# Seven accumulating DMAs in place of a matmul: summing the modulation rows of a decoder layer over partitions

## The chip, the cores and the metric

The kernel runs on one core of a Trainium2 chip. Its time is the device time of one execution in microseconds (us); where there are several runs the median is given. Engines are named as in the profile: PE is TensorE (its weight loads are PEld), DVE is VectorE, ACT is ScalarE, POOL is GpSimd, SP is SyncE, which here only issues DMAs. Each engine works through its own instructions in the order in which they were laid down; an instruction that waits holds up all behind it.

## The reference

One decoder layer on x of 512 tokens by 1024 channels. A modulation vector of 6 x 1024 numbers is computed from c; two of its parts scale and shift the first norm, one gates the first residual, two modulate the second norm, one gates the second residual.

```
mod = silu(c) @ w_ada + b_ada                    # 6 x 1024
shift1, scale1, gate1, shift2, scale2, gate2 = split(mod, 6)
h = rmsnorm(x, norm1_g) * (1 + scale1) + shift1
qa, ka, va, qd, kd, vd, ga, gd = split(h @ w_in)
out_a = sliding_window_attention(qa, ka, va, sinks)       # 8 heads of 64, window 128
out_d = diff_attention(qd, kd, vd, lam)                   # 4 heads, two softmax maps each
out_d = rmsnorm(out_d, subln_g) * 0.8                     # per head of 128 columns
merged = sigmoid(ga) * (out_a @ w_branch_swa) + sigmoid(gd) * (out_d @ w_branch_diff)
x = x + gate1 * (merged @ w_out)
h2 = rmsnorm(x, norm2_g) * (1 + scale2) + shift2
x = x + gate2 * conv_ffn(h2)
out = rmsnorm(x, final_g)
```

## The kernel before

All arithmetic is in float32. Large products are made of three matmuls: operands are split into a high part (a cast on ACT, L118) and a low part (a subtraction on DVE, L119), and high x high, high x low and low x high are summed in PSUM.

The kernel has four stages: the norm and the first 768 columns of the input projection (to about 56 us), the two attentions with the rest of the projections (to about 310 us), the output projection and second norm (to about 362 us), and the MLP. The change touches the second stage and the beginning of the third.

**How the second stage is laid out.** The order on PE is written by hand. Projections are cut into units; `fill(n)` (L539) issues n steps of three matmuls each of the current unit, and between the fills stand the attention's scores, transposes and values. `fill` also counts steps ("ticks"): every 8th tick it advances the generator `ada_rows` (L839), and functions put off with `after(n, fn)` run when their count is used up. `flush(kind)` (L569) runs what has been put into the list `beside[kind]`. On the other engines a scheduler decides the order when the kernel is built, by its own estimate of times and by priorities: `tc.high_priority(offset=HP)` moves instructions ahead (HP the most, HP // 2 less), `tc.issue_after(ins)` lets them follow an instruction. PSUM banks are taken by tag: "f" for projections (2), "s" for scores (3), "t" for transposes and small sums (2), "v" (1).

**Modulation rows.** The parts gate1, shift2, scale2 and gate2 (idx 0 to 3) are computed here, each in two halves of 512 (hf 0 and 1), so eight rows; I number them 0 to 7. For each row four loads of 512 KB bring 1024 x 512 weights (L835, `ra`, on SP, into buffers of the tag "raw" that all weight loads of this stage share, four in all), and DVE forms 8 products, each added to the one before (L857, L859, tile `arow`): 128 partitions x 512 partial sums. What remains is a sum over the 128 partitions. `ada_spread` (L872) does it on PE: four matmuls of a 128 x 32 block of ones with 128 columns of `arow`, side by side in the array (L876), fill a bank `pr`; ACT copies it (L881, `row`), and POOL writes 4 x 128 numbers to `mod_rows` in DRAM (L882). The partial sums have two buffers, tags "sq2" and "g2b1"; row 2 therefore takes the buffer of row 0.

**Sliding-window attention.** Four pairs of heads. `swa_scores` puts scores into banks, DVE adds the bias and takes the maxima (L620), `swa_softmax` takes exponentials on ACT (L635), adds the sink (L639, `lsum`), divides on DVE (L644), head j=0 then j=1; `swa_transpose` transposes the quotients on PE (L656, `tp`), ACT copies them (L658), `swa_values` multiplies (L666).

**Differential attention.** Sixteen blocks s = 4 h + n of 128 queries. Scores are read by DVE (L744), exponentials on ACT (L764), quotients of the two maps on DVE (L767 to L769); `diff_transpose` (L781, `td`), whose banks are read by ACT and DVE (L490, L491, `aTh`, `aTl`), and after the fourth block of a head `diff_values` (L124 `od`). The norm of a head: `stats` sums squares on PE (L804, `pss`), DVE forms the mean (L806 to L808, L181), POOL raises it to the power -0.5 (L185, `r`), DVE improves that (L193 to L195, `rt`, `drs`, L810); then `turn_norm` spreads the factors over columns on PE (L815, `rb`) and DVE multiplies (L816). `evac` (L488) reads the banks of q, k and v into the pair of high and low parts (L490, L491, L494).

**After the attention.** `brow` (L1066) loads a row broadcast to 128 partitions, on POOL's queue: gate1 with its bias into `g1b` (L1073, L1074), summed and halved on DVE (L1075, L1076) and multiplied into the output weights (L1105). `m2` gathers shift2, scale2, their biases and norm2_g (L1078 to L1080).

Of the kernel before, what the change touches and what calls it, by code (L numbers as in the profile page):

```python
# [28 lines left out]
ST = 6  # L29
ADA_LAG = 1  # L30
ADA_EVERY = 8
# [23 lines left out]
def kernel(  # L55
# [507 lines left out]

    beside = {"row": [], "sum": [], "norm": [], "turn": []}

    def after(n, fn):
        later.append([n, fn])
# [110 lines left out]
    def add_head(h):  # L678
        def q(wts):
            t = heads[h] = ap.tile([P, 6, S], F32R, tag="qkv", bufs=2, name=f"qkv{h}")  # L680
            o = fbank(f"pq{h}")
            yield from steps(o, wts, hT, KT)
            evac(t[:, 0], t[:, 1], o, 2.0 ** (2 * h - 1))

        def k(wts):
            t = heads[h]
            o = fbank(f"pk{h}")
            yield from steps(o, wts, hT, KT)
            evac(t[:, 2], t[:, 3], o)

        def v(wts):
# [7 lines left out]
            def turn():  # L699
                pv = tbank(f"pv{h}")  # L700
                for m in range(NT):
                    nc.tensor.transpose(pv[:, m * P : (m + 1) * P], vT[:, m * P : (m + 1) * P], ident)
                evac(t[:, 4], t[:, 5], pv)

# [81 lines left out]
    def diff_values(h):  # L786
# [14 lines left out]
        def stats():  # L801
# [37 lines left out]
    def ada_rows():  # L839
# [29 lines left out]
    spread = []  # L869


    def ada_spread(idx, hf, ac):  # L872
        pr = tbank(f"pr{idx}{hf}", (P, P))
        for g in range(4):
            gs = slice(32 * g, 32 * g + 32)
            nc.tensor.matmul(  # L876
                pr[gs], ones[:, gs], ac[:, g * P : (g + 1) * P], start=True, stop=True, tile_position=(0, 32 * g)
            )
        row = big.tile([P, P], F32, tag="g2b0", name=f"row{idx}{hf}")
        with tc.high_priority(offset=HP):  # L880
            spread.append(nc.scalar.copy(row, pr))  # L881
        nc.gpsimd.dma_start(  # L882
            mod_rows[idx, hf * S : (hf + 1) * S].rearrange("(g n) -> g n", g=4), row[0:P:32]
        )

# [3 lines left out]
    def add_gate_a(j):  # L889
# [5 lines left out]
        def load():  # L895
            if j % 2 == 0:
# [19 lines left out]

    group_ahead, sums = [1], {}
    pairs, firsts, scored, probs, aTs = {}, {}, {}, {}, {}
# [16 lines left out]
    for i in range(SWA_PAIRS):  # L935
        more = i + 1 < SWA_PAIRS
        fill(SWA_FILL[3])
        if more:
            flush("row")
            swa_scores(i + 1, range(NT))  # L940
# [10 lines left out]
        if i < 2:  # L951
            flush("row")
            swa_values(i)
        fill(SWA_FILL[7])
    while units or loaded or current:
        fill(1)
    flush("row")
    swa_values(2)
# [9 lines left out]
    for s in range(4 * DIFF_HEADS):  # L968
# [9 lines left out]
        if nxt:  # L978
            flush("row")
# [10 lines left out]
        if s == 13:  # L990
            group_ahead.clear()
        elif s > 13:
            flush("row")
        diff_softmax(*nxt)
# [3 lines left out]
    for j in range(4, KT):  # L998
        add_gate_a(j)
    fill(4)  # L1000
    flush("norm")
# [19 lines left out]
    def add_gate_d(j):  # L1021
# [6 lines left out]
        units.append((lambda: load_cols(win, COL_GD + j * P, f"wgd{j}"), gate))  # L1028

    def add_merge(j):  # L1030
        def load():
# [9 lines left out]
        def branch(wts):  # L1041
# [5 lines left out]
            nc.vector.tensor_add(td, td, ta[:, j])  # L1047
            split(mgh[j], mgl[j], td)

# [15 lines left out]

    def brow(dst, src):  # L1066
        nc.gpsimd.dma_start(dst, src.partition_broadcast(P))

# [9 lines left out]
    nc.gpsimd.dma_start(m2[0:16, :], mod_rows[1:3].rearrange("r (a p) -> (r a) p", p=P))  # L1078
    nc.gpsimd.dma_start(m2[16:32, :], b_ada[0, 3 * D : 5 * D].rearrange("(a p) -> a p", p=P))
    nc.gpsimd.dma_start(m2[32:40, :], norm2_g[0].rearrange("(a p) -> a p", p=P))  # L1080
    pm2 = tbank("pm2", (P, 40))
# [859 lines left out]
```

## Time and profile before

| | |
|---|---|
| Median of 3 runs | 691.77 us (691.5 to 693.38) |
| Profiled execution: time, span | 693.06 us, 691.3 us |
| Granted TensorE clock, mean | 0.996 |
| PE busy | 680.5 us, 98% of the span |
| DVE busy | 565.3 us, 82% |
| ACT busy | 384.6 us, 56% |
| POOL busy | 82.1 us, 12%, 100 instructions |
| DMA | 121.8 MB, q1 (issued by SP) 95.1 MB, q0 (issued by POOL) 25.7 MB |

A row of groups reads: line, engine, operation, tile written <- tiles read, shapes, count | busy time, mean of one | idle time before, and what ended it. A row of a timeline reads: start and duration in us, engine, line, operation, tiles, shapes, count, and in brackets the idle time before it and what ended it. A row of waits reads: engine, its tile and line <- what it waited for: us in total, times, longest. For a DMA, "landing" is the time from its issue until its data are confirmed.

### The profile page before, as it was taken

The page shows a single profiled execution, that of the slowest core. Times are in us where ns is not written, and L with a number is a line of the kernel's source. Part 1 is how long each engine was busy: PE and PEld are TensorE (multiplying, and loading weights), DVE is VectorE, ACT ScalarE, POOL GpSimd, SP SyncE. Part 2 cuts the span into 40 slices and gives each one's busy share as a digit, 9 for nine tenths or more (in the row PEclk, how much of TensorE's full clock was granted, in tenths as well). Part 3 has the DMA queues.
Part 4 walks back from the last instruction along what each step waited for, and adds up shares of the span by engine and source line. Part 5 has one row for each costly group of instructions (what it writes and reads, how often), then busy time and mean ns, then how long its engine had stood idle before and what let it go on. Part 6 is the DMA issues. An engine that isn't in the chain of part 4 may idle for free. (4 is left out here: it accounts for less than half of the span.)

```text
span 691.3 us, 11249 instructions
## 1 busy us (share of the span) xinstructions
PE 680.5 (98%) x4203; PEld 592.7 (86%) x4203; DVE 565.3 (82%) x1073; ACT 384.6 (56%) x686; POOL 82.1 (12%) x100
## 2 busy tenths in 40 slices
PE   8999999999999999999999999999999999999995
PEld 5787877788888888888889999999999999888884
DVE  5898987987885666663789988888888999979997
ACT  7676666545552323332477756655565666656665
POOL 3000000000001000000030101112111002540300
PEclk9999999999999999999999999999999999999998
DMA  9985454553455675229726798777978748997903
GB/s 307 328 258 165 140 156 151 154 163 96 138 138 169 212 217 180 91 95 315 230 56 129 166 214 197 167 173 215 206 215 217 155 149 207 196 195 199 167 1 121
DMA packets 115926, 121.81 MB, mean 176 GB/s; under 512 B 4447, under 2 KB 93344, under 8 KB 115872
## 3 DMA queue, kind: packets, MB, share of 16 engines
q1 hardware_dynamic: 96958, 95.09, 43.8%
q0 software_dynamic: 18720, 25.73, 22.2%
q8 instruction: 33, 0.54, 0.3%
q10 hardware_dynamic: 194, 0.28, 0.1%
q14 instruction: 21, 0.17, 0.1%
HBM read 118.97 MB, written 2.11 MB: 175 GB/s over the span
## 5 line engine op out<-in xcount | busy, mean ns | idle before, releaser
L1270 PE MATMUL up<-t,m_whi 128*128 128x256 f32 x512 | 93.1, 283 | 0.0
L1270 PEld LDWEIGHTS up<-t,m_whi 128*128 128x128 f32 x512 | 79.9, 192 | 0.0
L1270 PE MATMUL up<-t,m_wlo 128*128 128x256 f32 x256 | 72.4, 283 | 0.0
L1270 PE MATMUL up<-bh,p_whi 128*128 128x256 f32 x232 | 65.7, 283 | 0.0
L1270 PE MATMUL up<-bl,p_whi 128*128 128x256 f32 x232 | 65.7, 283 | 0.0
L1270 PE MATMUL up<-bh,p_wlo 128*128 128x256 f32 x232 | 65.7, 283 | 0.0
L859 DVE SCALAR_TENSOR_TENSOR arow<-ra,cs,arow 128x512 f32<-128x512 f32 x56 | 42.0, 749 | 20.0 <-DMA ra<-in_w_ada_dram 19.4
L1270 PEld LDWEIGHTS up<-t,m_wlo 128*128 128x128 f32 x256 | 49.2, 192 | 0.0
L1270 PEld LDWEIGHTS up<-bh,p_whi 128*128 128x128 f32 x232 | 44.5, 192 | 0.0
L1270 PEld LDWEIGHTS up<-bl,p_whi 128*128 128x128 f32 x232 | 44.5, 192 | 0.0
L1270 PEld LDWEIGHTS up<-bh,p_wlo 128*128 128x128 f32 x232 | 44.5, 192 | 0.0
L1179 POOL DMA_DIRECT2D s<-in_w_up_dram x21 | 27.0, 1361 | 140.8 <-DMA s<-in_w_up_dram 66.5
L1207 ACT CAST m_whi<-s 128x1024 fp32r<-128x1024 f32 x31 | 32.5, 1049 | 11.1 <-DVE s L1201 6.3
L1211 DVE TENSOR_TENSOR m_wlo<-s,m_whi 128x1024 fp32r<-128x1024 f32 x31 | 37.8, 1219 | 0.0
L1270 PE MATMUL up<-t,p_whi 128*128 128x256 f32 x176 | 32.2, 283 | 0.0
L882 POOL DMA_DIRECT2D mod_rows<-row x8 | 4.9, 614 | 204.9 <-ACT row L881 204.9
L1270 PEld LDWEIGHTS up<-t,p_whi 128*128 128x128 f32 x176 | 27.5, 192 | 0.0
L1277 ACT ACTIVATE gT<-a,cv 128x512 f32<-128x512 f32 x22 | 17.8, 816 | 16.9 <-DVE a L1312 15.8
L185 POOL TENSOR_TENSOR r<-ms,mhalf 128x1 f32<-128x1 f32 (+1 forms) x16 | 12.6, 791 | 120.9 <-DVE ms L183 73.1
L1207 ACT CAST p_whi<-wa 128x1024 fp32r<-128x1024 f32 x18 | 18.8, 1046 | 12.5 <-PE up L1270 12.5
L1211 DVE TENSOR_TENSOR p_wlo<-wa,p_whi 128x1024 fp32r<-128x1024 f32 x18 | 22.0, 1223 | 3.8 <-ACT p_whi L1207 3.8
L1270 PE MATMUL up<-t,p_wlo 128*128 128x256 f32 x88 | 24.9, 283 | 0.0
(491 smaller groups left out, 2064.9 us busy)
## 6 DMA issues: line engine op xcount, KB each, us to landing
ra<-in_w_ada_dram SPq DMA_DIRECT2D x32, 512.0 KB, 4.4
wa<-in_w_up_dram SPq DMA_DIRECT2D x22, 512.0 KB, 3.9
s<-in_w_up_dram SPq DMA_DIRECT2D x21, 512.0 KB, 4.5
s<-in_w_up_dram POOLq DMA_DIRECT2D x21, 512.0 KB, 6.6
adaw<-in_w_ada_dram SPq DMA_DIRECT2D x12, 512.0 KB, 7.6
w<-in_w_in_dram SPq DMA_DIRECT2D x12, 512.0 KB, 4.9
a<-in_w_up_dram SPq DMA_DIRECT2D x11, 512.0 KB, 4.5
b<-in_w_down_dram SPq DMA_DIRECT2D x10, 512.0 KB, 4.6
```

Of the source, the lines that this page charges most:

```text
L185: nc.gpsimd.tensor_tensor(r0, ms, mhalf[:, :n], ALU.pow)
L859: nc.vector.scalar_tensor_tensor(ac, r[:, a], cc, ac, ALU.mult, ALU.add)
L882: nc.gpsimd.dma_start(mod_rows[idx, hf * S : (hf + 1) * S].rearrange("(g n) -> g n", g=4), row[0:P:32])
L1179: nc.gpsimd.dma_start(dst, upblock(*blk), accum_op=ALU.add)
L1207: nc.scalar.copy(W[J, name][0], R[J, SRC[name]])
L1211: nc.vector.tensor_sub(lo, R[J, SRC[name]], hi.bitcast(F32))
L1270: nc.tensor.matmul(o[u], w[:, k, cu], b[:, k], start=name in ("p1", "m5", "p2") and k == 0 and x == 0, stop=k == 3 and x == 2, skip_group_ ...
L1277: nc.scalar.activation(grow(j), av[J][:, u], AF.Identity, bias=cv[:, 66 + j : 67 + j], scale=cv[:, 44 + j : 45 + j])
```

## The change

The sum over partitions of each modulation row is made by DMAs that accumulate, issued by POOL: the upper half of the partitions is added to the lower half, seven times (64, 32, ... 1 partition), and the first partition is written to `mod_rows`. The matmuls, the bank, ACT's copy and the lists that timed them are gone. The partial sums have three buffers in turn, so row 3 takes the buffer of row 0. The readings of the q and k banks are given a priority of HP * 3 // 4, which lies above that of the rows' products (HP // 2); those of the v bank and the multiplication with the norm factors get HP. The norm factors of the heads before the last are spread two steps after the transposes of a head's second block, where they were spread after the first block's scores had been issued; those of the third head come two steps later. `g1b` and the constant parts of `m2` are loaded on SP's queue, and `g1b` is summed after the second block of the merge. The split of the first branch weights no longer follows a copy of a row.

```diff
-                ac = big.tile([P, S], F32, tag=("sq2", "g2b1")[hf], name=f"arow{idx}{hf}")
+                ac = big.tile([P, S], F32, tag=("sq2", "g2b1", "g2b0")[(2 * idx + hf) % 3], name=f"arow{idx}{hf}")
...
             if k == KT - 2:
-                row = lambda idx=idx, hf=hf, ac=ac: ada_spread(idx, hf, ac)
-                if group_ahead:
-                    beside["row"].append(row)
-                else:
-                    after(ADA_LAG, row)
+                ada_sum(idx, hf, ac)
...
-    def ada_spread(idx, hf, ac):
-        pr = tbank(f"pr{idx}{hf}", (P, P))
-        for g in range(4):
-            gs = slice(32 * g, 32 * g + 32)
-            nc.tensor.matmul(
-                pr[gs], ones[:, gs], ac[:, g * P : (g + 1) * P], start=True, stop=True, tile_position=(0, 32 * g)
-            )
-        row = big.tile([P, P], F32, tag="g2b0", name=f"row{idx}{hf}")
-        with tc.high_priority(offset=HP):
-            spread.append(nc.scalar.copy(row, pr))
-        nc.gpsimd.dma_start(
-            mod_rows[idx, hf * S : (hf + 1) * S].rearrange("(g n) -> g n", g=4), row[0:P:32]
-        )
+    def ada_sum(idx, hf, ac):
+        n = P // 2
+        while n:
+            nc.gpsimd.dma_start(ac[0:n], ac[n : 2 * n], accum_op=ALU.add)
+            n //= 2
+        nc.gpsimd.dma_start(mod_rows[idx : idx + 1, hf * S : (hf + 1) * S], ac[0:1])
...
             yield from steps(o, wts, hT, KT)
-            evac(t[:, 0], t[:, 1], o, 2.0 ** (2 * h - 1))
+            with tc.high_priority(offset=HP * 3 // 4):
+                evac(t[:, 0], t[:, 1], o, 2.0 ** (2 * h - 1))
...
-                nc.vector.tensor_mul(of, of, rb)
+                with tc.high_priority(offset=HP):
+                    nc.vector.tensor_mul(of, of, rb)
...
-                with tc.issue_after(spread[-1].ins) if j == 0 else ExitStack():
-                    pair_w["a"] = split_pair(r, [P, 4, 2 * P], f"wba{j}")
+                pair_w["a"] = split_pair(r, [P, 4, 2 * P], f"wba{j}")
...
         if n == 1:
             diff_transpose(s)
-        fill(DIFF_FILL[2] + ahead)
+            fill(2)
+            flush("norm")
+        fill(DIFF_FILL[2] + ahead - 2 * (n == 1))
         if n == 2:
             flush("sum")
-        elif n == 0:
-            flush("norm")
...
-    fill(4)
+    fill(6)
     flush("norm")
...
-    brow(g1b, mod_rows[0])
-    brow(g1bias, b_ada[0, 2 * D : 3 * D])
-    nc.vector.tensor_add(g1b, g1b, g1bias)
-    nc.vector.tensor_scalar_mul(g1b, g1b, 0.5)
+    brow(g1b, mod_rows[0], nc.sync)
+    brow(g1bias, b_ada[0, 2 * D : 3 * D], nc.sync)
+    with tc.issue_after(merged[1][1].ins):
+        nc.vector.tensor_add(g1b, g1b, g1bias)
+        nc.vector.tensor_scalar_mul(g1b, g1b, 0.5)
     m2 = bp.tile([40, P], F32, name="m2")
+    nc.sync.dma_start(m2[16:32, :], b_ada[0, 3 * D : 5 * D].rearrange("(a p) -> a p", p=P))
+    nc.sync.dma_start(m2[32:40, :], norm2_g[0].rearrange("(a p) -> a p", p=P))
     nc.gpsimd.dma_start(m2[0:16, :], mod_rows[1:3].rearrange("r (a p) -> (r a) p", p=P))
```

More of the change, by code (lines that the diff above doesn't have):

```diff
@@ L29 @@
 ST = 6
-ADA_LAG = 1
 ADA_EVERY = 8
@@ L562, in fill @@
                 next(ada, None)
-    beside = {"row": [], "sum": [], "norm": [], "turn": []}
+    beside = {"sum": [], "norm": [], "turn": []}
     def after(n, fn):
@@ L688, in k @@
             yield from steps(o, wts, hT, KT)
-            evac(t[:, 2], t[:, 3], o)
+            with tc.high_priority(offset=HP * 3 // 4):
+                evac(t[:, 2], t[:, 3], o)
         def v(wts):
@@ L702, in turn @@
                     nc.tensor.transpose(pv[:, m * P : (m + 1) * P], vT[:, m * P : (m + 1) * P], ident)
-                evac(t[:, 4], t[:, 5], pv)
+                with tc.high_priority(offset=HP):
+                    evac(t[:, 4], t[:, 5], pv)
             if h:
@@ L815, in turn_norm @@
                     nc.tensor.transpose(rb[:, n * P : (n + 1) * P], rs[:, n : n + 1].to_broadcast([P, P]), ident)
-                nc.vector.tensor_mul(of, of, rb)
+                with tc.high_priority(offset=HP):
+                    nc.vector.tensor_mul(of, of, rb)
                 split(outd[0][:, h], outd[1][:, h], of)
@@ L915, in add_gate_a @@
         units.append((load, branch))
-    group_ahead, sums = [1], {}
+    sums = {}
     pairs, firsts, scored, probs, aTs = {}, {}, {}, {}, {}
@@ L938 @@
         if more:
-            flush("row")
             swa_scores(i + 1, range(NT))
@@ L951 @@
         if i < 2:
-            flush("row")
             swa_values(i)
@@ L956 @@
         fill(1)
-    flush("row")
     swa_values(2)
@@ L978 @@
         if nxt:
-            flush("row")
             diff_scores(*nxt)
@@ L982 @@
             diff_transpose(s)
-        fill(DIFF_FILL[2] + ahead)
+            fill(2)
+            flush("norm")
+        fill(DIFF_FILL[2] + ahead - 2 * (n == 1))
         if n == 2:
             flush("sum")
-        elif n == 0:
-            flush("norm")
         if n != 1:
             diff_transpose(s)
[L990 to L993, printed above, removed]
         diff_softmax(*nxt)
@@ L1028, in add_gate_d @@
         units.append((lambda: load_cols(win, COL_GD + j * P, f"wgd{j}"), gate))
+    merged = []
     def add_merge(j):
@@ L1047, in branch @@
             nc.vector.tensor_add(td, td, ta[:, j])
-            split(mgh[j], mgl[j], td)
+            merged.append(split(mgh[j], mgl[j], td))
         units.append((load, branch))
@@ L1063, with brow @@
     man.close()
-    def brow(dst, src):
-        nc.gpsimd.dma_start(dst, src.partition_broadcast(P))
+    def brow(dst, src, q=nc.gpsimd):
+        q.dma_start(dst, src.partition_broadcast(P))
     TAIL = 3
```

3 lines of the change are left out of this document (removed).

## The prediction

> **What bounds the kernel now.** I read the page first (engine shares, chain), then TensorE's waits in the stretch the change touches (56 to 345 us), then the timelines of single engines there.
>
> ```profile
> span 691.3 us, 11249 instructions
> PE 680.5 (98%) x4203; PEld 592.7 (86%) x4203; DVE 565.3 (82%) x1073; ACT 384.6 (56%) x686; POOL 82.1 (12%) x100
> PE tp L656 <- DVE st L644: 0.5, 1, 0.5
> 125.00:150.00 25.00, 25.00 (x138) 19.84 (x137) 22.12 (x63) 13.88 (x35) 0.58 (x1) 1.00 0.55 166
> 225.00:250.00 25.00, 25.00 (x119) 20.30 (x118) 15.79 (x20) 8.49 (x11) 2.13 (x4) 1.00 0.69 217
> ```
>
> TensorE is busy for 98% of the span. In the third line, the only row of its waits between 56 and 345 us, it waits once, 0.5 us, for the softmax quotients of the last window pair. So two things count: TensorE work removed is worth its own length, and anything that makes VectorE late can only cost. The last two lines are stretches of 25 us (busy TensorE, its weight loads, VectorE, ScalarE, POOL, the granted clock, the DMA share): VectorE has room after 200 us (15.79 of 25) but little where softmax feeds transposes (22.12). The time is made against the profiled execution's own 693.06 us, which lies 1.29 above the median 691.77; I give the time as the median plus the sum.
>
> **Removed from TensorE.** Eight groups of eight records (four matmuls each), with their copies.
>
> ```profile
> L876 PE MATMUL pr<-arow,ones x64: 272/285/298, 108.9 to 283.7; 128*32 128x128 f32 x64
> 131.65 0.39 PE L123 MATMUL pA<-outal,wba_h 128*128 128x512 f32 x1
> 131.87 0.40 PE L124 MATMUL pA<-outah,wba_l 128*128 128x512 f32 x1
> 132.20 0.43 PE L876 MATMUL pr<-arow,ones 128*32 128x128 f32 x8
> 132.55 0.95 PE L129 MATMUL sd<-qkv 64*128 64x128 f32 x12
> ```
>
> By starts, a group holds TensorE 0.35 us (132.20 to 132.55), and the matmul ahead takes 0.33 instead of 0.22 us before the next start. Eight times 0.35, and 0.1 for the five groups that follow a projection: 3.3 us off the bound engine. The eight copies leave ScalarE, which is busy for 56%: nothing.
>
> **Row 2 no longer waits for TensorE, and so stands in front of the last softmax.** Before, the third row shared a buffer with the first, and its first product waited until 109.42 for the first row's matmuls. With three buffers that wait is gone, and in the changed kernel's order on VectorE the row's products come earlier:
>
> ```
> arow(row 1) last two | row 2: product 1, 2 | lsum, recip, st x4 (head j=0)
> | row 2: product 3 | lsum (j=1) | row 2: product 4 | recip | qkv<-pk | st x4 (j=1)
> ```
>
> ```profile
> 99.24 0.37 SPq L835 DMA_DIRECT2D ra<-in_w_ada_dram  x1
> ra<-in_w_ada_dram SPq DMA_DIRECT2D x1, 512.0 KB, 4.2
> 102.33 0.37 SPq L835 DMA_DIRECT2D ra<-in_w_ada_dram  x1
> 100.77 1.54 DVE L859 SCALAR_TENSOR_TENSOR arow<-ra,cs,arow 128x512 f32<-128x512 f32 x2
> 103.03 0.16 DVE L639 TENSOR_TENSOR lsum<-lsum,es 128x4 f32<-128x4 f32 x1 [0.73 <-ACT st L635]
> 106.49 0.69 DVE L491 TENSOR_TENSOR qkv<-pk,qkv 128x512 fp32r<-128x512 f32 x1
> 109.42 0.48 DVE L857 TENSOR_SCALAR arow<-ra,cs 128x512 f32<-128x512 f32 x1 [2.24 <-PE pr L876]
> 103.88 1.13 PE L656 MATMUL tp<-ident,st 128*128 128x128 f32 x7 [0.49 <-DVE st L644]
> 106.25 0.93 PE L656 MATMUL tp<-ident,st 128*128 128x128 f32 x7
> ```
>
> Nothing on VectorE, ScalarE or TensorE differs up to 102.3, so row 2's first load is still issued at 99.24 and lands 4.2 us later, at 103.44. VectorE, in order, stands in front of product 1 until then; products 1 and 2 take it to 104.7 and the sum of 103.03 follows 1.6 us late. That goes straight to TensorE, which already waited here: the transposes of 103.88 move to 105.5. The second load is issued at 102.33; by the same 4.2 it lands at 106.5, somewhat sooner if it has the engines alone; product 3 starts at 106.2 to 106.5, and products 3 and 4 and the reading of the k bank (0.69, now ahead) put the second head's quotients at 108.4 to 109.4. TensorE, with six matmuls (1.4 us) between, reaches the second transposes at 107.9 instead of 106.25 and is done with them at 109.6, not 106.93. Cost 2.7 us; bounds 1.5 (loads already there, VectorE work alone) and 3.4 (the chain's 128 KB beside the second load). I take 2.7, since the issue times are rows.
>
> Row 2's last load can only be issued when its third pair of products frees a buffer, which is now later against the softmax of blocks 2 and 3.
>
> ```profile
> 129.58 0.62 DVE L769 SCALAR_TENSOR_TENSOR sd<-sd,dls,sd 128x384 f32<-128x384 f32 x1
> 130.35 0.52 PE L781 MATMUL td<-ident,sd 128*128 128x128 f32 x3
> ```
>
> The quotient ends at 130.20 and TensorE transposes at 130.35: no slack. In the new order some 2.6 us of softmax work stand between that pair and the load's first use, against 4.2 of landing: VectorE is 1.6 late there. It regains 0.8, since the last product (0.7) no longer stands between exponentials and this quotient: 0.8 us, bounds 0 and 1.6.
>
> **The accumulating DMAs.** Each row: seven transfers of 128, 64, ... 2 KB within SBUF, each issued by POOL only when the one before has landed, then the write to mod_rows. 64 DMAs instead of 8, 2.0 MB in all against 121.8. POOL issues in order, and it also computes the `pow` for the heads' norm factors, for which VectorE waits in order.
>
> ```profile
> L882 POOL DMA_DIRECT2D mod_rows<-row x8: 541/604/771, 110.1 to 284.6; - x8
> DMA to landing us min/median/max: 1.6/3.1/4.2
> DMA to landing us min/median/max: 1.8/1.8/1.8
> DMA to landing us min/median/max: 4.2/4.2/4.2
> DMA to landing us min/median/max: 1.7/1.7/1.7
> DMA to landing us min/median/max: 1.6/1.6/1.6
> 239.95 0.60 POOL L882 DMA_DIRECT2D mod_rows<-row  x1 [4.67 <-ACT row L881]
> 241.90 0.50 POOL L1078 DMA_DIRECT2D m<-mod_rows  x1 [1.35 <-DMA mod_rows<-row]
> q0 software_dynamic: 18720, 25.73, 22.2%
> ```
>
> The nearest rows are POOL's eight small writes, all of them and then four by their own windows (at 110, 193, 240 and 262 us): issue to landing 1.6 to 4.2, median 3.1. After one (landing 1.7) POOL resumed at 241.90, so 0.25 us to resume: a step costs 1.85 to 4.45, by the median 3.35. Queue 0's packets: 22.2% of 16 x 691.3 over 18720 is 0.13 us for 1.4 KB, so 0.2 for 2 KB; 64 rows on 16 engines add 0.6 to the first step, 0.2 to the second.
>
> The Trainium skill (DMA: Bandwidth & Descriptors, section Anatomy of one DMA — SWDGE (gpsimd) path) puts a DMA from this engine at 2.0 us plus its bytes over 436 GB/s, most of it the receipt, heaviest for HBM. By it a step is 2.0 to 2.3 us, nothing on POOL is late, and the sum ends at +0.2 instead of +2.2. The trace agrees for three of the eight writes (1.6 to 1.8); with the median at 3.1 the others took half as long again and more.
>
> Where the `pow`s stand in POOL's new order decides. The third one stands behind six transfers of row 4.
>
> ```profile
> 189.23 0.75 DVE L859 SCALAR_TENSOR_TENSOR arow<-ra,cs,arow 128x512 f32<-128x512 f32 x1
> 202.67 1.03 POOL L185 TENSOR_TENSOR r<-ms,mhalf 128x4 f32<-128x4 f32 x1 [9.10 <-DVE ms L181]
> 205.46 0.15 DVE L194 TENSOR_TENSOR rt<-rt,ms 128x4 f32<-128x4 f32 x1
> 207.66 0.68 DVE L491 TENSOR_TENSOR aTl<-td,aTh 128x512 fp32r<-128x512 f32 x1
> 208.53 0.39 PE L123 MATMUL od<-aTl,qkv 128*128 128x512 f32 x1
> ```
>
> Row 4 is complete at 189.98. Five steps at 3.35 plus 0.8, the sixth issue (0.6) and the `pow` (1.03) end at 209.2, where VectorE wants it at 205.5. From there to the end of the bank read aTl are 3.1 us: 212.3. The values matmul that needs it, at 208.53 before, stands six matmuls (1.4) later and 0.45 earlier for the group removed: 209.5. So 2.8 late by the median, 0 by 1.85 a step. The write at 193 lies in this very stretch and took 4.2. I take 2.0, nearer the upper end.
>
> The first `pow` stands behind three chains and one step:
>
> ```profile
> 79.05 0.75 DVE L859 SCALAR_TENSOR_TENSOR arow<-ra,cs,arow 128x512 f32<-128x512 f32 x1
> 154.81 1.04 POOL L185 TENSOR_TENSOR r<-ms,mhalf 128x4 f32<-128x4 f32 x1 [20.96 <-DVE dr L806]
> 155.88 0.16 DVE L193 TENSOR_TENSOR rt<-r 128x4 f32<-128x4 f32 x1 [0.87 <-POOL r L185]
> ```
>
> Chain 0 starts at 79.8; with a step s a chain is 7s + 1.4, and the `pow` ends at 79.8 + 3(7s + 1.4) + s + 2.2, wanted at 155.88 plus the 2.7 lost earlier. That holds up to s = 3.3. The three quick writes give 1.95 a step; for a step beside loads I take 3.9, between the median's 3.35 and the slowest's 4.45. One of each kind, at the DMA share of 0.55, is some 2.9 each: in time, so nothing here. What a late one costs is shortened by the slack before the next transposes:
>
> ```profile
> 160.49 0.35 DVE L769 SCALAR_TENSOR_TENSOR sd<-sd,dls,sd 128x128 f32<-128x128 f32 x1
> 162.26 0.27 PE L781 MATMUL td<-ident,sd 128*128 128x128 f32 x1
> ```
>
> The quotient is done at 160.84, TensorE takes it at 162.26: 1.4 us. The second and fourth `pow` stand behind finished chains: nothing.
>
> **Moved or free.** The norm transposes stand two fills later (some 1.4 us), in front of nothing that waits; they cover part of a late `pow`. g1b's two loads and m2's two small ones move from POOL to SP behind row 6's loads; VectorE's idle third covers the 1 MB, else one row load is 3 us late, bounds 0 and 1. g1b's sum (1.2 and 0.7 us) lies in the same idle time. Row 7's chain ends some 30 us after its row, at about 295 us; its reader belongs to the MLP's middle. ScalarE's split of the first branch weights comes some 4 us earlier, in front of one bank copy: one cast, some 1 us, while TensorE is late there anyhow: nothing. The higher priority of the q, k and v bank reads shows in the order only at the k bank counted above.
>
> **Sum.** -3.3 + 2.7 + 0.8 + 2.0 = +2.2: 694.0 (695.3 against the profiled execution's own time). What a measurement can tell from no change is 0.3%, 2.1 us: 689.7 to 693.8.
>
> **Rivals.**
> - Faster: TensorE's 3.3 us are kept. It decides at the last window pair: if TensorE's stall there grows by less than 1.2 us (the loads land in 3 us, or the softmax was less tight than the 0.5 us wait says) and the `pow`s are in time, the time is 688.5 to 689.7. Against it speak the two issue times; for it, that TensorE waits nowhere else. 0.17.
> - The steps are cheap (1.85 us, the idle landing): no `pow` is late, the row 2 loss stays: -3.3 + 2.7 + 0.8 = +0.2, 692.0. For it the landings of 1.6 to 1.8, against it the median of 3.1. By the rule above it would be this. 0.15.
> - The chain is the bound: above 3.3 us a step each 0.1 makes the first `pow` 2.2 later, 1.4 of it covered by the time until the next transposes. At 3.6: 6.6 late, 5.2 on TensorE, 699.4; at 3.8 about 704. For it, the median step is 3.35; against it, that a stretch between loads halves it. 0.28.
>
> **Chances.** My forecast has 0.40, its own range 692.5 to 697, a third of it below 693.8. Slower: 0.28 and 0.27, together 0.55; same: 0.13 and 0.15, with rounding 0.27; faster 0.18. The range 688.7 to 704 leaves out the best of the first rival and the tail of the last.
>
> **What would show it.** TensorE's waits: tp for st between 103 and 110 grown from 0.5 to about 3 us. VectorE waiting for ra at 102.3 and 106. rt for r with over 2 us at 205 and under 1 at 156. The accumulating transfers landing in 2.9 us on average; no pr group. Wrong if rt waits 5 us or more at 156 (third rival), or tp keeps its 0.5 (first).

## The result, and the profile after

The changed kernel takes 699.83 us (median of 17 runs, 693.85 to 703.94), the kernel before 692.28 beside it (17 runs, 691.5 to 693.38): ratio 1.0105, interval 1.0083 to 1.0128, slower by 7.3 us. The forecast was 694.0 with 688.7 to 704.0. The range holds the time, the sign is right, and the size is three times and more what I gave. The profiled execution took 698.35 us, somewhat less than the median. Single runs spread over 10 us, those of before over 2; that is the first sign that something irregular decides.

Lines have moved a little: a row's products are now L860 and L862 (before L857, L859), the accumulating transfers L871, the write L873, `tp` L655, `td` L783, `rb` L817, POOL's `pow` L184.

The page of the changed kernel:

```profile
span 696.5 us, 11182 instructions
PE 678.9 (97%) x4139; PEld 592.6 (85%) x4139; DVE 565.0 (81%) x1073; ACT 381.7 (55%) x678; POOL 123.3 (18%) x152
```

The waits of TensorE from 56 to 345 us, where before had one of 0.5 us (columns: us in total, times, longest; one of 0.3 is left out):

```profile
PE tp L655 <- ACT qkv L489: 2.3, 1, 2.3
PE td L783 <- DVE dls L769: 1.5, 1, 1.5
PE od L122 <- DVE aTl L490: 1.4, 1, 1.4
PE rb L817 <- DVE drs L812: 1.3, 1, 1.3
PE rb L817 <- DVE qkv L490: 0.8, 1, 0.8
PE td L783 <- DVE qkv L490: 0.5, 1, 0.5
```

TensorE has 64 matmul records less, and is busy 1.6 us less. The six waits shown are 7.8 us, with the one left out 8.1, instead of 0.5. The first is the last window pair's transposes (the releaser named is a cast that ended in the same moment; in E5 below the same wait names the quotients). The second stands behind the first `pow`, the third and fourth behind the third.

The waits of VectorE and then of POOL in the same stretch say where these come from:

```profile
DVE arow L862 <- DMA ra<-in_w_ada_dram: 28.4, 14, 5.5
...
DVE rt L192 <- POOL r L184: 10.5, 4, 4.4
DVE arow L860 <- DMA arow<-arow: 4.5, 2, 2.5
```

```profile
POOL arow L871 <- DMA arow<-arow: 129.4, 48, 5.8
```

`rt` waits for POOL's `pow` 10.5 us in four waits, where it was 4.4. The four cost about 1.1 each where nothing is late; two of them now take 3.9 and 4.4. POOL itself stands 129 us in front of the chains' own transfers. The third row of VectorE names the chains, but it is hardly a wait for their buffers: it is the first product of rows 4 and 5 (at 168.70 and 197.96), which take the buffers of rows 1 and 2, and these were written out at 130.14 and 151.10. The loads of their weights were issued on SP only at 164.34 and 193.32, some 4.5 us before.

Row 2 at the last window pair, on VectorE's timeline:

```profile
102.79 0.49 DVE L860 TENSOR_SCALAR arow<-ra,cs 128x512 f32<-128x512 f32 x1 [1.17 <-DMA ra<-in_w_ada_dram]
...
103.98 0.16 DVE L638 TENSOR_TENSOR lsum<-lsum,es 128x4 f32<-128x4 f32 x1
...
105.57 0.75 DVE L862 SCALAR_TENSOR_TENSOR arow<-ra,cs,arow 128x512 f32<-128x512 f32 x1
...
107.69 1.07 DVE L643 TENSOR_SCALAR st<-st,lsum 128x128 f32<-128x128 f32 x4
```

That is the order predicted: VectorE stands in front of product 1 until the load has landed, two products go ahead of the first head's sum, the other two ahead of the second head's quotients.

The chains on POOL's timeline. Row 0's chain begins at 79.26 and writes at 106.00, row 1's runs from there to 130.14, row 2's to 151.10; row 3's starts at 153.30, and the first `pow` stands behind its second issue. Row 4's sixth issue stands in front of the third `pow`:

```profile
79.26 1.02 POOL L871 DMA_DIRECT2D arow<-arow  x1 [67.64 <-DVE lsum L639]
106.00 0.52 POOL L873 DMA_DIRECT2D mod_rows<-arow  x1 [2.00 <-DMA arow<-arow]
...
130.14 0.52 POOL L873 DMA_DIRECT2D mod_rows<-arow  x1 [2.92 <-DMA arow<-arow]
...
151.10 0.52 POOL L873 DMA_DIRECT2D mod_rows<-arow  x1 [1.88 <-DMA arow<-arow]
153.30 0.81 POOL L871 DMA_DIRECT2D arow<-arow  x1 [1.68 <-DVE arow L862]
159.22 0.76 POOL L871 DMA_DIRECT2D arow<-arow  x1 [5.11 <-DMA arow<-arow]
159.75 1.30 POOL L184 TENSOR_TENSOR r<-ms,mhalf 128x4 f32<-128x4 f32 x1
...
212.21 0.79 POOL L871 DMA_DIRECT2D arow<-arow  x1 [3.54 <-DMA arow<-arow]
212.75 1.33 POOL L184 TENSOR_TENSOR r<-ms,mhalf 128x4 f32<-128x4 f32 x1
```

Seven steps took 26.7, 23.6 and 20.5 us: 3.8, 3.4 and 2.9 a step, 3.4 on average (the write's 0.5 lies between). The prediction's limit for the first `pow` was 3.3, and the step of row 3 behind which it stood took 5.9 (153.30 to 159.22). What VectorE saw of it (the first line is row 3's last product, the second the mean that the first `pow` takes):

```profile
152.26 0.75 DVE L862 SCALAR_TENSOR_TENSOR arow<-ra,cs,arow 128x512 f32<-128x512 f32 x1
...
156.80 0.16 DVE L180 TENSOR_SCALAR ms<-dr 128x4 f32<-128x4 f32 x1
...
161.08 0.16 DVE L192 TENSOR_TENSOR rt<-r 128x4 f32<-128x4 f32 x1 [3.85 <-POOL r L184]
...
214.11 0.16 DVE L192 TENSOR_TENSOR rt<-r 128x4 f32<-128x4 f32 x1 [4.38 <-POOL r L184]
```

So the three long chains did not hold the first `pow` up here: they had ended at 151.6, before row 3 was complete at 153.0. What did was the first step of row 3, 128 KB, alone: the mean was ready at 157.0, POOL reached the `pow` at 159.75.

In the profiled execution the account is: 3.3 saved, against 7.6 us more of waits and some 1.5 us of half clock after the first of them (last section): +5.8, where the two profiled executions differ by 5.3 (698.35 - 693.06).

### The profile page after: what moved, and what is told of

It is laid out like the page before. It is cut to its first block, busy times and chain, and to the rows that moved or that the text cites. A ratio compares the mean times of both kernels' runs of the same rounds, so it can differ in the third digit from the quotient of the medians.

```text
span 696.5 us, 11182 instructions
## 1 busy us (share of the span) xinstructions
PE 678.9 (97%) x4139; PEld 592.6 (85%) x4139; DVE 565.0 (81%) x1073; ACT 381.7 (55%) x678; POOL 123.3 (18%) x152
## 4 chain that ended last, share of the span: by engine, by line
PE 70%; DMA 13%; DVE 12%; issue 2%; ACT 2%; POOL 1%; SPq 0%; POOLq 0%; DVEq 0%; ACTq 0%
PE up L1253 32%; PE dc L1868 15%; DMA ra<-in_w_ada_dram 8%; PE a L384 5%; DVE arow L862 4%; DMA arow<-arow 3%; PE oc L1309 2%; PE oc L1313 2%; PE oc L1310 2%; DVE st L619 1%; DVE sd L746 1%; DVE wga_l L118 1%; PE pgd L123 1%; PE pgd L121 1%; PE pgd L122 1%
## 5 line engine op out<-in xcount | busy, mean ns | idle before, releaser
L871 POOL DMA_DIRECT2D arow<-arow x56 | 44.7, 802 | 219.0 <-DMA arow<-arow 129.4
L862 DVE SCALAR_TENSOR_TENSOR arow<-ra,cs,arow 128x512 f32<-128x512 f32 x56 | 42.0, 749 | 29.1 <-DMA ra<-in_w_ada_dram 28.4
L184 POOL TENSOR_TENSOR r<-ms,mhalf 128x1 f32<-128x1 f32 (+1 forms) x16 | 13.2, 825 | 82.7 <-DVE ms L182 73.0
L766 ACT ACTIVATE sd<-sd,dmx 128x128 f32<-128x128 f32 (+3 forms) x32 | 17.6, 554 | 17.2 <-DVE dmx L756 17.2
```

Of the source, the lines that this page charges most:

```text
L766: exp = nc.scalar.activation(pm[m], pm[m], AF.Exp, bias=mx[:, m : m + 1], scale=slope, accum_out=ls)
L862: nc.vector.scalar_tensor_tensor(ac, r[:, a], cc, ac, ALU.mult, ALU.add)
L871: nc.gpsimd.dma_start(ac[0:n], ac[n : 2 * n], accum_op=ALU.add)
```

## The experiments

The theory after the result: two costs in series on VectorE's order, row 2's early products and `pow`s that stand on POOL behind chains that have not ended. Rivals: the chains' transfers slow other traffic; the moved steps (norm transposes, priorities, loads on SP) carry part of it. Each run was timed beside the kernel before, and the ratio is to that. The groups of runs were on different chips, so between groups the ratios are compared, or medians where that is said.

| | edit | median, us | ratio to before |
|---|---|---|---|
| E1 | before, third row buffer | 695.47 | 1.0031 (1.0017 to 1.0046) |
| E2 | changed, row 2's first products held | 703.0 | 1.0109 (1.0062 to 1.0156) |
| E3 | changed, `pow`s in front | 696.5 | 1.0053 (1.0037 to 1.0070) |
| E4 | E2 and E3 | 696.74 | 1.0055 (1.0041 to 1.0068) |
| E5 | changed, no `pow` on POOL | 691.79 | 0.9983 (0.9973 to 0.9993) |
| E6 | changed, no chains | 690.91 | 0.9972 (0.9962 to 0.9982) |
| E7 | before, moved steps alone | 693.24 | 1.0009 (1.0000 to 1.0017) |
| E8 | before, chains for rows 4 to 7 behind the last `pow` | 695.33 | 1.0049 (1.0030 to 1.0067) |
| E9 | E8, loads on SP | 696.53 | 1.0047 (1.0029 to 1.0065) |
| E10 | changed, all orders kept | 698.16 | 1.0067 (1.0047 to 1.0086) |
| E11 | E9, chains in turn | 697.84 | 1.0071 (1.0054 to 1.0088) |
| E12 | E10, chains in turn, split held | 695.84 | 1.0040 (1.0023 to 1.0056) |

### E1: row 2's early products alone

```
-  ac = big.tile([P, S], F32, tag=("sq2", "g2b1")[hf], ...)
+  ac = big.tile([P, S], F32, tag=("sq2", "g2b1", "g2b0")[(2 * idx + hf) % 3], ...)
-  row = big.tile([P, P], F32, tag="g2b0", ...)
+  row = big.tile([P, P], F32, tag="rowp", ...)
```

> The kernel before, with a third buffer for the rows and nothing else: row 2's products come early as in the changed kernel (two of them ahead of the last window pair's first sum), but the rows are still summed on TensorE. My theory (the early products stand for 2.7 to 3.4 us of the loss): 2.5 to 3.5 us slower than before, about 695, and TensorE's wait for the last pair's quotients grows from 0.5 to 2 to 3 us. Rival (VectorE's order there is covered, and the stall of the changed kernel comes from the transfers beside the load): within 1 us of before.

Slower by 0.31%, 2.1 us (1.2 to 3.2), somewhat less than the 2.5 to 3.5 expected. TensorE's waits of E1 in the stretch, and VectorE in front of product 1:

```profile
PE tp L656 <- DVE st L644: 2.6, 2, 1.9
```

```profile
104.28 0.49 DVE L857 TENSOR_SCALAR arow<-ra,cs 128x512 f32<-128x512 f32 x1 [1.09 <-DMA ra<-in_w_ada_dram]
```

The early products cost this without any chain: TensorE waits 2.1 us more for the quotients than before.

### E2, E3, E4: take the one cause away, the other, both

```
 E2:
+            elif (idx, hf) == (1, 0) and k in (0, 2):
+                hold = tc.issue_after(pairs[SWA_PAIRS - 1].divided.ins)
 E3: (pows: the heads' pow instructions so far; a chain waits until its number of them is laid down)
+    BEHIND, pows, waiting = {3: 1, 4: 3, 5: 4}, [], []
...
+        with tc.issue_after(pows[-1].ins) if pows else ExitStack():
+            nc.gpsimd.dma_start(ac[0:n], ac[n : 2 * n], accum_op=ALU.add)
```

> The changed kernel, with row 2's first two products held behind the last window pair's last quotient. Theory (two costs in series: the early products, then `pow`s that stand on POOL behind the chains, whose end does not move): the stall at 102 goes, but TensorE is then 3 us earlier at the heads while the first `pow` ends when it did, so most comes back as a longer wait at 156 to 165: 0 to 1.5 us off the changed kernel, about 698.5 to 700, and the times of single runs spread over as many us as before the edit. Rival (the costs add up, each where it stands): 3 us off, about 696.5.

> The changed kernel, with the chains of rows 2, 3, 4 and 5 each issued behind the `pow` that stands before them in time, so that no `pow` stands behind a chain that has not ended; row 2's early products stay. Theory: the first `pow` (1.3 us late on TensorE in the profiled run) and the third (3.9) are in time: 691.5 to 693.5, and the spread of single runs falls from 10 us to about 2. Rival (the extra transfers slow other traffic, or the moved norm steps cost): 696 or more, and the spread stays.

> Both edits on the changed kernel. Theory: only the eight groups off TensorE are left of the change, 3.3 us: 688.5 to 690, faster than the kernel before by 0.3 to 0.5%. If the costs do not interact, this is the sum of the two edits' gains alone; by the theory it is more than the sum, by 1.5 to 3 us. Rival (moved steps or traffic cost something too): 691 or more.

E2 is no faster than the changed kernel: 703.0, above the 698.5 to 700 expected, with single runs again spread over 10 us (694.28 to 704.51). The theory's reason is not what its profile shows. TensorE waits 1.1 us at 104 to 107 instead of 2.3, but two waits at the first blocks, 0.5 us before, take that back and more:

```profile
PE td L783 <- DVE sd L771: 1.5, 1, 1.5
PE td L783 <- DVE qkv L490: 1.4, 1, 1.4
```

So it does not come to the heads earlier, as the theory had it. The waits at the `pow`s are longer in that execution (`rt` up to 6.2 us).

E3 gains half (1.0105 to 1.0053) and its runs lie within 3.5 us, but it stays 3 us above the 691.5 to 693.5 expected. E4 should have gained all, and gained nothing over E3. (The 1.3 and 3.9 us of E3's expectation are 1.5 and 2.7 by the waits above.) Two things had taken the place. The first on VectorE's timeline of E4, the second on that of E3:

```profile
117.58 0.75 DVE L870 SCALAR_TENSOR_TENSOR arow<-ra,cs,arow 128x512 f32<-128x512 f32 x1 [3.68 <-DMA ra<-in_w_ada_dram]
...
123.98 0.75 DVE L870 SCALAR_TENSOR_TENSOR arow<-ra,cs,arow 128x512 f32<-128x512 f32 x1 [1.59 <-DMA ra<-in_w_ada_dram]
```

```profile
229.98 0.16 DVE L194 TENSOR_TENSOR rt<-r 128x4 f32<-128x4 f32 x1 [5.39 <-POOL r L186]
```

Holding products 1 to 4 frees their buffers later, so row 2's next loads come later, and products 5 and 7 now wait for them in front of the softmax of the first blocks: TensorE waits 2.8 us there in E4 (1.6 and 1.2, for the quotients and the bank read behind them). And row 4's chain, sent behind the third `pow`, is not done when the fourth is wanted: for the fourth, in time before, VectorE now waits 5.4 us (1.2 of them as ever). The rival of E2 (costs add up, 696.5) fell; that of E3 and E4 (traffic, moved steps) was not excluded, since E4 came out 7 us above its expectation.

### E5, E6: the chain with nothing behind it, and no chain

E5 keeps every chain and puts a VectorE operation in place of the heads' `pow`; E6 leaves the accumulating transfers out. Neither computes the layer; they only show times.

```
 E5:
-        nc.gpsimd.tensor_tensor(r0, ms, mhalf[:, :n], ALU.pow)
+        if n > 1: nc.vector.tensor_scalar(r0, ms, 1.0, 1.0, ALU.min, ALU.mult)
+        else:     nc.gpsimd.tensor_tensor(r0, ms, mhalf[:, :n], ALU.pow)
 E6:
-        while n:
-            nc.gpsimd.dma_start(ac[0:n], ac[n : 2 * n], accum_op=ALU.add)
-            n //= 2
```

> The changed kernel with all its chains, but the heads' four `pow`s are replaced by a 0.2 us operation on VectorE (min with 1; the norm factors are wrong and the output is not the reference's), so that VectorE never waits for POOL there; VectorE's order is otherwise that of the changed kernel. It separates what a chain costs through the `pow` behind it from all else that it could cost. Theory (late `pow`s are the second cost, and the fourth one, late by the edit, is why holding them in front brought no more): the stalls after 155 go, also those at 240 and 275; what is left is row 2's 2.5 to 3 us, 0.5 to 1 before 132, and the 3.3 saved: 692 to 693.5, single runs within 3 us of each other. Rival (row 6's loads and the moved norm steps cost by themselves): the stalls at 240 and 275 stay, 695 or more.

> The changed kernel without its 56 accumulating transfers (the sum over partitions is left out; only the write of one partition to mod_rows stays). Theory (transfers cost only through the `pow`s): the same as with chains and no `pow` on POOL, within 1 us, 691.5 to 693.5. Rival (traffic of the chains and waits for their buffers cost too): 1.5 us or more below the run with chains and no `pow`.

TensorE's waits of E5 from 56 to 345 us that reach 0.3:

```profile
PE tp L658 <- DVE st L646: 1.8, 1, 1.8
PE td L786 <- DVE qkv L493: 0.7, 1, 0.7
```

These two runs decide. With all 56 transfers and their traffic, but no `pow` of the heads on POOL behind them, the kernel is 0.17% faster than before, 8.0 us below the changed kernel by the medians (8.4 by the ratios), and its ten runs lie within 2.2 us. Without the transfers it is only 0.9 us lower still. So of the 56 transfers' cost some 8 us go through the `pow`s and about 1 through all else; the traffic rival falls. (E6 keeps the four `pow`s, E5 has none; but in E6 VectorE waits 4.3 us for them, as before, and no wait of TensorE comes of it.) What is left against the 3.3 saved is row 2's wait at 104 and 0.7 at the first blocks, as expected. The stalls at 240 and 275 of E3 are gone. That they too came from the late fourth `pow` is likely, not shown: VectorE there also waited 4.6 us for a load, and E5 differs from E3 in the order of the chains as well.

### E7: the moved steps alone

The edits to the kernel before, in brief (the reads of the k and v banks and of `rb` get priorities likewise, m2's two small loads go to SP likewise):

```
-            evac(t[:, 0], t[:, 1], o, 2.0 ** (2 * h - 1))
+            with tc.high_priority(offset=HP * 3 // 4):
+                evac(t[:, 0], t[:, 1], o, 2.0 ** (2 * h - 1))
...
-        elif n == 0:
-            flush("norm")
+            fill(2)                      # after diff_transpose of n == 1
+            flush("norm")
...
-    brow(g1b, mod_rows[0])
+    brow(g1b, mod_rows[0], nc.sync)
...
+    with tc.issue_after(merged[1][1].ins):
+        nc.vector.tensor_add(g1b, g1b, g1bias)
```

> The kernel before with only the rest of the change: the higher priority of the bank reads, the norm transposes two fills later, the loads of g1b and m2 on SP; rows are summed on TensorE with two buffers. My prediction priced all of it at nothing: 691.5 to 693.5. Rival (these steps carry part of the loss, as the stalls at 240 and 275 would have it): 694 or more, with stalls of TensorE after 190.

Slower by 0.09% (0.00 to 0.17): 0.6 us, 1.2 at most. TensorE waits 2.1 us instead of 0.5, 1.1 at the transposes at 130 and 1.0 at those at 202. The moved steps do not carry the loss.

### E8 to E12: a version that keeps the gain

E8, on the kernel before (`waiting` holds the rows until the fourth `pow` is laid down):

```
+                if idx > 1:
+                    ada_sum(idx, hf, ac)
-                if group_ahead:
+                elif group_ahead:
...
+        if len(pows) < 4:
+            waiting.append((idx, hf, ac)); return
+        n = P // 2
+        while n:
+            with tc.issue_after(pows[-1].ins):
+                nc.gpsimd.dma_start(ac[0:n], ac[n : 2 * n], accum_op=ALU.add)
+            n //= 2
```

E9, on E8, and E11, on E9:

```
-    brow(g1b, mod_rows[0])
+    brow(g1b, mod_rows[0], nc.sync)
...
-            with tc.issue_after(pows[-1].ins):
+            with tc.issue_after((written or pows)[-1].ins):     # E11; written: the writes to mod_rows so far
```

E10, on E4, and E12, on E10:

```
-    BEHIND, pows, waiting = {3: 1, 4: 3, 5: 4}, [], []
+    BEHIND, pows, waiting = {3: 1, 4: 4, 5: 4, 6: 4, 7: 4}, [], []
...
+            elif (idx, hf) == (1, 0) and k in (4, 6):
+                hold = tc.issue_after(lasts[1]) if len(lasts) > 1 else ExitStack()
...
+            with tc.issue_after(written[-1].ins) if written else ExitStack():      # E12
...
+                with tc.issue_after(c.copied.ins) if j == 0 else ExitStack():      # E12; c: the last window pair
                     pair_w["a"] = split_pair(r, [P, 4, 2 * P], f"wba{j}")
```

> The kernel before, with the chains for rows 4 to 7 alone, all of them behind the fourth `pow` and with a third buffer for row 6; rows 0 to 3 are summed on TensorE as before, and VectorE's order is the one of before up to row 6. Theory (a chain costs nothing where no compute of POOL stands behind it): four groups less on TensorE, 4 x 0.4 = 1.6 us, 690.0 to 691.5, 0.1 to 0.3% faster than before. Rival (chains cost by their traffic): 692 or more.

> As the chains behind the last `pow` (rows 4 to 7 alone, on the kernel before), with the loads of g1b, its bias and m2's two small ones on SP, and g1b's sum behind the second merge, as the change has them. In the run without this, POOL issued the bias's load at 239.8 between the chains' transfers, VectorE waited 4.7 us for it and TensorE 3.7. Theory (POOL's queue is the only cost of a chain, whatever stands behind it, DMAs as well as compute): that stall goes, and four groups less on TensorE show: 690.5 to 691.8, 0.1 to 0.35% faster than before. Rival (the stall moves to another load or step): 693 or more.

> The changed kernel with every cost found taken away by order alone: rows 2 and 3 issue their chains behind the first and the second `pow` or later, rows 4 to 7 behind the fourth; row 2's first two products stand behind the last window pair's last quotient, and its later ones behind the quotient of blocks 0 and 1, as in the kernel before. Theory (early products and POOL's queue are all that the change costs): 3.3 us less than before less what is left of small waits, 688.7 to 690.3, faster by 0.3 to 0.6%. Rival (VectorE's order gives back at the next softmax what it saves, as it did when only the first two products were held): 691.5 to 693.

> As the late chains with loads on SP, but each chain starts only when the one before it is written, so that they no longer interleave. In the run without this, rows 4 and 5 took turns on POOL, both ended near 262, and row 7's first product waited 6.5 us for the buffer of row 4; TensorE lost 4.9 at the branch merges of 269 to 275. Theory (a chain costs by what waits behind it: compute, a load, and a buffer): row 4's buffer is free near 245, that stall goes, four groups less on TensorE show: 690.5 to 692, 0.1 to 0.35% faster than before. Rival (chains cost somewhere in any order): 694 or more.

> As the run with all orders kept, with the chains one after another for the same reason (there row 7's first product waited 8.6 us for row 4's buffer, TensorE 6.3), and ScalarE's split of the first branch weights behind the last window pair's copies, where it stood before (it stood ahead of them there and TensorE waited 0.75 at 107). Theory: nothing of the change's cost is left, only its eight groups off TensorE: 689 to 691, 0.25 to 0.6% faster than before. Rival (row 2's products cost at the last window pair wherever they stand, or a chain does): 692.5 or more.

All five missed by 4 to 8 us, each mostly by one stretch of waits, and none beats the kernel before. In E8 the `pow`s are all in time, but the load of g1b's bias is issued by POOL too. POOL, VectorE and TensorE of E8, one row each:

```profile
239.81 1.02 POOL L1088 DMA_DIRECT2D xn<-in_b_ada_dram  x1
```

```profile
245.69 1.23 DVE L1096 TENSOR_TENSOR g1b<-g1b,xn 128x1024 f32<-128x1024 f32 x1 [4.67 <-DMA xn<-in_b_ada_dram]
```

```profile
250.02 0.50 PE L122 MATMUL pgd<-hThA,wgd_h 128*128 128x512 f32 x1 [3.68 <-DVE ta L933]
```

With that load on SP (E9), and in E10 to E12, the next one shows: row 7's first product takes the buffer of row 4, whose chain now starts at 220 and has not ended. POOL, VectorE and TensorE of E12:

```profile
220.53 0.86 POOL L889 DMA_DIRECT2D arow<-arow  x1
...
251.74 0.52 POOL L894 DMA_DIRECT2D mod_rows<-arow  x1 [4.52 <-DMA arow<-arow]
```

```profile
253.54 0.48 DVE L871 TENSOR_SCALAR arow<-ra,cs 128x512 f32<-128x512 f32 x1 [8.99 <-DMA mod_rows<-arow]
```

```profile
272.61 0.80 PE L123 MATMUL pB<-outdA,wbd 128*128 128x512 f32 x1 [3.92 <-DVE wbd L118]
```

VectorE stands 9 us; the splits of the branch weights behind it are late, and TensorE loses 5.5 us (1.6 and 3.9) and runs at half clock for a while. In E9 and E10 the same wait is 6.5 and 8.6 us. In E11 it is 6.9, but the profile names no releaser for it. Running the chains one by one instead of interleaved did not take the wait away: row 4's chain took 31 us for its seven steps, 4.5 each. (The expectations of E11 and E12 have some numbers too high: in E9's profile rows 4 and 5 are written at 253.7 and 254.6, not near 262, and TensorE loses 4.3 us there and 5.5 in E10.) E11 is no faster than E9. E12 is faster than E10, but holds the split too, and their intervals overlap. Up to there E12 keeps the gain. The same two places on TensorE's timeline, before and E12 (the start of a window pair's scores, and the first gate of the second branch):

```profile
92.51 0.44 PE L129 MATMUL sw<-ka,qa 64*128 64x128 f32 x4
242.75 0.39 PE L122 MATMUL pgd<-hThA,wgd_h 128*128 128x512 f32 x1
```

```profile
91.25 0.44 PE L128 MATMUL sw<-ka,qa 64*128 64x128 f32 x4
239.04 0.39 PE L121 MATMUL pgd<-hThA,wgd_h 128*128 128x512 f32 x1
```

150.24 us before, 147.79 in E12: 2.45 us gained over the stretch that holds six of the eight groups, 0.41 each, with five chains started by then. TensorE's waits in the stretch are 0.5 us in both, so the gain is that of the groups. So up to 240 next to nothing of the change's costs is left when the orders are kept; what is then left is a buffer. A fourth one for row 7 was not tried, so that a version faster than before exists is argued, not shown.

## Why the prediction was right or wrong

**Eight groups off TensorE, -3.3: right.** Worked out as 0.41 each, measured 0.41 in E12, over six of them.

**Row 2 in front of the last softmax, +2.7 (1.5 to 3.4): right.** 2.1 (1.2 to 3.2) in E1 by time. In the changed kernel the wait grew from 0.5 to 2.3 us, where "about 3" was said, and a stretch at half clock stands behind it, where E6, at full clock, has a second wait of 0.7. The order, the wait for the load and the quotients' times came as worked out.

**Row 2's last load, +0.8 (0 to 1.6): right in kind, small.** It showed one softmax earlier, 0.5 us at the first blocks, 0.7 in E5; nothing in E1. In E4, with later loads, it became 2.8, and 2.9 in E2.

**The third `pow`, +2.0 (0 to 2.8): the place right, the size at the upper end.** VectorE waits 4.4 us, TensorE 1.3 and 1.4: 2.7 in the profiled execution. The five steps (193.59 to 212.21) took 3.7 each, where 3.35 was worked with.

**The first `pow`, 0: wrong, and the step that failed.** It waited 3.9 us on VectorE, and TensorE 1.5. The prediction set one value, 2.9, for all the steps ahead of it ("One of each kind, at the DMA share of 0.55, is some 2.9 each: in time"). Two things were wrong with that. The mean over the first three chains was 3.4; the nearest row, the median landing of 3.1 (3.35 with the resume), would have said so, and I had mixed it with idle steps of 1.95, where the shortest here, from an issue to the next, is 2.2. But that was not yet the cause: by the prediction's own formula 3.4 makes the `pow` 2.2 us late, with 1.4 covered, and in the profiled execution the three chains had in fact ended 1.4 us before row 3 was complete. The formula left out that row 3's chain cannot start before its products are done. From there the `pow` had only one step in front of it, and that step, the first of a chain with 128 KB, took 5.9 us (6.6 in E2, 6.5 in E5). It alone accounts for the 2.7 us by which the `pow` was late. So the term that was mis-sized is this single step: 2.9, with 0.6 for its size, where 5.9 was measured.

**The third rival (0.28, 699.4 at 3.6 a step): near by luck.** The median is 699.83, but its mechanism, 21 steps too long in a row, is not what the profile shows, and its sign, `rt` waiting 5 us or more at 156, did not come: it waited 3.9. Much of the loss came from the third `pow` and from what follows a stop.

**All `pow`s together: 2.0 predicted, 8.0 measured** (changed kernel less E5, medians). The two profiled executions differ by 5.9 (698.35 - 692.46), of which 4.2 are direct waits of TensorE at the first and third `pow`. The one execution with a profile is on the faster side of the seventeen. In these the mean granted clock is 0.989 to 0.994 in the ten above 699.5 and 0.993 to 0.998 in the seven below, and in E2's profile of 704.51 us the clock is halved after the `pow`s' waits (last section). So half clock is likely to be part of the rest; how much is open.

**The second and fourth `pow`, 0: right.** Their waits are 1.1 and 1.2, as before. E3 shows how near that was: with row 4's chain 13 us later, VectorE waits 5.4 us for the fourth.

**The quick steps, rival of 692.0: wrong**, and with it the rule of the Trainium skill (DMA: Bandwidth & Descriptors, section Anatomy of one DMA — SWDGE (gpsimd) path). 2.0 us plus bytes over 436 GB/s gives 2.0 to 2.3 us from issue to landing. The changed kernel's chains have these, by size, as medians of eight, in the view of DMA issues, and for all 56 together in the view of their line:

```profile
arow<-arow POOLq DMA_DIRECT2D x8, 128.0 KB, 4.9
arow<-arow POOLq DMA_DIRECT2D x8, 64.0 KB, 3.0
arow<-arow POOLq DMA_DIRECT2D x8, 32.0 KB, 2.2
...
arow<-arow POOLq DMA_DIRECT2D x8, 2.0 KB, 2.3
```

```profile
DMA to landing us min/median/max: 1.9/2.9/6.3
```

Some of the small ones agree; the largest is twice as long, and the longest of all is nearly three times the rule.

**Moved or free, 0: right within 0.6 us** for the steps of E7 (0 to 1.2). ScalarE's split, costed at nothing "while TensorE is late there anyhow", is free only for that reason: in E10, where TensorE is in time, it makes TensorE wait 0.6 us for the copies behind it, and in E12, with the split held, that wait is gone. **Buffer reuse by the chains** was costed at nothing, and in the changed kernel no wait for a buffer shows; with the chains moved later, in E9 to E12, it is the largest cost of all.

**The faster rival** (0.17) fell at the place named for it, the last window pair. Once the late `pow`s are gone, as in E5 and E6, there is a gain of 0.2 to 0.3%, 1.2 and 1.9 us. The 3.3 saved less the waits left in their profiles (2.2 and 2.6 us more than before) would be 1.1 and 0.7.

## What to carry to other kernels

A chain of dependent transfers issued by an engine that also computes is to be costed by everything that stands behind it in that engine's order: the compute, the loads, and the buffers that it keeps; here each in turn held VectorE up, 4 to 9 us a time, while the traffic itself cost about 1. Ask first from when the chain counts: the first `pow` was decided not by the 21 steps before but by the one step after row 3 was complete. A computation that stands behind few steps wants their size and the longest time of their kind under load, not a mean over all steps. When a product is held back because it is too early, its load is held back too, and the wait comes back at the next place, unless the products there are held as well (E10, E12).

## What was not expected of the hardware

**A short stop of TensorE can cost more than its length.** Windows of 2 us (busy TensorE, weight loads, VectorE, ScalarE, POOL, granted clock, DMA share, GB/s): the changed kernel 2 us after its 2.3 us wait, and E2 after the third `pow`:

```profile
106.00:108.00 2.00, 2.00 (x6) 1.56 (x6) 2.00 (x7) 0.64 (x2) 1.36 (x2) 0.50 0.75 214
```

```profile
220.00:222.00 2.00, 0.85 (x4) 0.34 (x3) 2.00 (x3) 0.00 (x0) 0.52 (x1) 0.50 0.02 1
```

```profile
106.00:108.00 2.00, 1.31 (x9) 0.72 (x8) 2.00 (x8) 0.00 (x0) 0.00 (x0) 1.00 0.39 117
```

In the first the granted clock is 0.50 and a 512-column matmul starts every 0.43 us instead of 0.23. In E2, after waits of 3.0 and 1.2 us, it stays at 0.50 for some 6 us; in the changed kernel, after 1.3 and 1.4 at the same place, it stayed at 1.00. The third row is E6: its wait at the same place was 2.0 us and the clock stayed at 1.00. The Trainium skill (TensorE: Matmul & The Clock Gate, section Part 1: The HAM clock gate (the "warmup" mystery)) has two states, full and half, and a free-running window of about 3.4 us without work as the way down. The runs agree on the half; a wait of 2.3 us was enough here, and in E5 one of 1.8 (0.50 in the same window), while 2.0 in E6 and in E3 was not. None of these waits is as long as the window that the page gives. The length alone does not decide, as a free-running window would have it.

**The chain's pace goes with the DMA share beside it.** In the changed kernel rows 0 to 2 took 2.9 to 3.8 us a step at a DMA share of 0.54 to 0.61, and row 5 took 4.8 at 0.78 (228.85 to 262.50); in E12 row 4 took 4.5 at 0.73. VectorE's busy share does not order them the same way: 0.87 beside row 0, 0.54 beside row 5, the slowest. What makes a step slow was not tested.
